# The adaLN matrix-vector product of a two-block kernel, moved to TensorE

## The chip, the cores and the metric

One Trainium2 chip, of which the kernel uses one core. The metric is the device time of one execution in microseconds (us). The kernel before takes 2879.64 us, the median of three runs (2877.4 to 2880.94).

## The reference

Two transformer blocks run one after the other on one sequence of 512 tokens with 1024 features, all in float32. The change concerns the first block alone, and in it the six conditioning vectors (adaLN), which come from one row `c` and a 1024 x 6144 matrix:

```python
ada = jax.nn.silu(c) @ w_ada + b_ada
shift1, scale1, gate1, shift2, scale2, gate2 = jnp.split(ada, 6, axis=-1)
h = modulate(rms_norm(x, norm1_g), shift1, scale1)      # h * (1 + scale) + shift
proj = h @ w_in + b_in                                  # attention and convolution branches
x = x + gate1[:, None, :] * mix
h2 = modulate(rms_norm(x, norm2_g), shift2, scale2)
x = x + gate2[:, None, :] * peer_layer(h2, ...)
```

Behind that come the PEER layer (a search over 16384 experts), and a second block with a Hyena filter, neighbourhood attention, pooling and a mixture of 16 experts.

## The kernel before

Activations are kept transposed: `X` holds 8 chunks of 128 features (partitions) by 512 tokens. So each of the 6 x 8 = 48 pieces of `ada` is a column of 128 numbers, used as a per-partition scale or shift. The host lays `w_ada` out in 24 groups of 1 MB. A group gives two columns of `ada`; for the first eight groups these are the shift and the scale of one feature chunk k.

`ada_group(g)` (L201) makes two columns. `c`, broadcast to all 128 partitions, stands in `cb` [128 x 1024] with the SiLU applied. Partition p of the group's tile holds the 1024 weights of output feature p, twice. For the first column, VectorE multiplies by `cb` and sums in one pass (L205). For the second, GpSimd multiplies (L206) and ScalarE sums while it copies (L207). VectorE adds the bias (L208). No TensorE instruction takes part.

`ada_load(g)` (L191) says where a group lies: groups 0 to 3 in the tiles `wide`, which later hold the filter's tables and the `mh`/`ml` of the output projection, group 6 in the room of `q_sb`, all others in two rotating buffers `wada`. All are loaded on SyncE's queue, which also carries `w_in`, `w_out` and all later weights, in order.

Around it the first block runs in these stages:

- The first stage loads `X`, forms the RMS norm (`nps`, `rps`), and then, chunk by chunk for k = 0 to 7: `ada_group(k)`, the scale `gs` (L233), `modulate` (L166 to L170: `mt` on VectorE, `mt` again and `hh` on ScalarE, `hl` on VectorE), and 15 matmuls that add chunk k to five blocks of the input projection in PSUM. Each product is made of three (`mm3`, L84): `hh` and `hl` are the high and low parts of the activations, `whi` and `wlo` those of the weights, which ScalarE and VectorE split (L81, L82).
- The second stage makes the Hyena filters of the second block (`hyena_filters`, two sine steps that pass between VectorE, ScalarE and TensorE) and the first attention scores (`ssp`, one PSUM tile of two banks) with their softmax.
- The third stage holds the other 13 blocks of the input projection, four attention blocks (`pt`, `op`, `nps`, `rps`), four convolution groups, `ada_group` 8 to 23, and the output projection (`mh`, `ml`).
- Behind it come a filter spectrum (`dw` loaded, L437), the second norm and the PEER layer.

The order of instructions inside these stages is not the order of the program. A scheduler puts each engine's instructions in an order of its own from the dependences, the buffers and a cost table. Each engine then runs its list strictly in that order; the same holds for SyncE's loads. Only the main loop of the PEER layer is written out by hand (`manual_schedule`).

Of the kernel before, what the change touches and what calls it, by code (L numbers as in the profile page):

```python
# [9 lines left out]
F32 = mybir.dt.float32  # L10
# [4 lines left out]
AF = mybir.ActivationFunctionType  # L15
ALU = mybir.AluOpType
# [4 lines left out]
P = 128  # L21
D = 1024
KD = 8
T = 512
# [11 lines left out]
def body(ctx, tc, I, O):  # L36
    nc = tc.nc
    mm = nc.tensor.matmul
    act = nc.scalar.activation
    vtt = nc.vector.tensor_tensor  # L40
    vts = nc.vector.tensor_scalar
    stt = nc.vector.scalar_tensor_tensor
    ptt = nc.gpsimd.tensor_tensor
# [4 lines left out]
    def const(name, shape, src=None, q=None, pool=None):  # L48
        t = (pool or cp).tile(shape, F32, name=name, tag=name)
        (q or nc.sync).dma_start(t, I[name] if src is None else src)  # L50
        return t
# [11 lines left out]
    ident = const("ident", [P, P], q=nc.scalar)  # L63
    ones = const("ones", [P, P], q=nc.scalar)
    hblk = const("hblk", [P, P], q=nc.scalar)
    cols = const("cols", [P, I["cols"].shape[1]], q=nc.scalar)
    eps_t = cp.tile([P, 1], F32, name="eps_t", tag="eps_t")
    nc.vector.memset(eps_t, EPS)
# [7 lines left out]
    def cols_of(name):  # L76
        o, n = CO[name]
        return cols[:, o:o + n]
# [83 lines left out]
    ada = cp.tile([P, 48], F32, name="ada", tag="ada")  # L162
# [14 lines left out]
    with ExitStack() as fx:  # L177
        fp = fx.enter_context(tc.tile_pool(name="fp", bufs=1))
        pp = fx.enter_context(tc.tile_pool(name="fps", bufs=2, space=PSUM))

        def mmp():
            return pp.tile([P, T], F32, name="mmp", tag="mmp", bufs=3)

        cb = fp.tile([P, D], F32, name="cb", tag="cb")
        a = I["c"]
        nc.scalar.dma_start(cb, bass.AP(tensor=a.tensor, offset=a.offset, ap=[[0, P], [1, D]]))
        act(cb, cb, AF.Silu)

        wide = [fp.tile([P, 2, 2, D], F32, name="wide", tag=tag) for tag in ("mh", "ml")]

        def ada_load(g):  # L191
            if g < 4:
                w = wide[g // 2][:, g % 2]
            elif g == 6:
                w = fp.tile([P, 2, D], F32, name="wq", tag="q_sb")
            else:
                w = fp.tile([P, 2, D], F32, name="wada", tag="wada", bufs=2)
            nc.sync.dma_start(w, I["w_ada"][g])
            return w

        def ada_group(g, w=None):  # L201
            if w is None:
                w = ada_load(g)
            b = 2 * g
            stt(w[:, 0], w[:, 0], 1.0, cb, op0=ALU.mult, op1=ALU.mult, accum_out=ada[:, b:b + 1])  # L205
            ptt(w[:, 1], w[:, 1], cb, op=ALU.mult)  # L206
            act(w[:, 1], w[:, 1], AF.Copy, accum_out=ada[:, b + 1:b + 2])  # L207
            vtt(ada[:, b:b + 2], ada[:, b:b + 2], cols_of("b_ada")[:, b:b + 2], op=ALU.add)  # L208

        hh = fp.tile([P, KD, T], F32R, name="hh", tag="hh")  # L210
        hl = fp.tile([P, KD, T], F32R, name="hl", tag="hl")
# [4 lines left out]
        with ExitStack() as ex:  # L216
            ep = ex.enter_context(tc.tile_pool(name="ep", bufs=1))
            ws0 = WStream(ep, I["w_in"], bufs=3, per=1, hbufs=NI)
            s1 = ep.tile([P, T], F32, name="s1", tag="s1")
            act(s1, X[:, 0], AF.Square)  # L220
            for k in range(1, KD):
                vtt(s1, s1, square(ep, X[:, k]), op=ALU.add)
            r1 = rms_t(ep, pp, [s1], D, False)
            wf, aw = [], []
            for i in range(4):
                wf += [ws0.get(b) for b in range(2 * i, min(2 * i + 2, NI))]
                aw.append(ada_load(i))
            early = [mmp() for _ in range(3)] + [pp.tile([P, T], F32, name="mmp", tag="pt", bufs=2) for _ in range(NI - 3)]
            for k in range(KD):
                ada_group(k, aw[k])  # L230
                if k + 4 < KD:
                    aw.append(ada_load(k + 4))
                stt(gs1[:, k:k + 1], ada[:, 2 * k + 1:2 * k + 2], 1.0, cols_of("norm1_g")[:, k:k + 1],  # L233
                    op0=ALU.add, op1=ALU.mult)
                modulate(k, r1, gs1[:, k:k + 1], ada[:, 2 * k:2 * k + 1], hh, hl, fp)
                for b in range(NI):
                    mm3(early[b], wf[b][0][:, k], wf[b][1][:, k], hh[:, k], hl[:, k], k == 0, k == KD - 1)
            q_sb = fp.tile([P, 4, T], F32, name="q_sb", tag="q_sb")
            for i in range(NI):
                act(q_sb[:, i] if i < 4 else k_sb, early[i], AF.Identity, bias=col("b_in", i))  # L240

        hyena_filters(nc, fp, mmp, I, pm)
        mh = fp.tile([P, KD, T], F32R, name="mh", tag="mh")
        ml = fp.tile([P, KD, T], F32R, name="ml", tag="ml")
# [5 lines left out]
        ps = mmp()  # L250
# [71 lines left out]
        for i in range(4):  # L322
            sc = attn_scores(i)
            conv_group(i)
            attn_out(*sc)
            if i == 1:
                for g in range(8, 12):
                    ada_group(g)
# [3 lines left out]
        for g in range(12, 20):  # L332
            ada_group(g)
        for i in range(KD):
            ps = mmp()
# [1034 lines left out]
def prep(inp):  # L1370
    g = {k: np.asarray(v) for k, v in inp.items()}
    A = {}

    def colv(v):
        return v.reshape(-1, P).T
# [3 lines left out]
        return w.reshape(KD, P, n, per, P).transpose(2, 1, 3, 0, 4)  # L1379

    A["xT"] = g["x"][0].T.reshape(KD, P, T).transpose(1, 0, 2)
    A["c"] = g["c"].reshape(1, D)
    A["ident"] = np.eye(P, dtype=np.float32)
    A["ones"] = np.ones((P, P), np.float32)
    A["hblk"] = np.kron(np.eye(2), np.ones((64, 64))).astype(np.float32)
    starts = [0, 16, 24, 32, 40, 44, 48, 52] + list(range(56, 64))
    A["start_row"] = np.tile(np.array(starts, np.float32), (P, 1))
    ao = np.array([k + 8 * s for k in range(8) for s in range(2)] + list(range(16, 48)))
    A["w_ada"] = g["w_ada"].T.reshape(48, P, D)[ao].reshape(24, 2, P, D).transpose(0, 2, 1, 3)
    hperm = [h for i in range(4) for h in (i, i + 4)]  # L1390
    qperm = np.concatenate([np.arange(64) + 64 * h for h in hperm])
    cgrp = [np.concatenate([1280 + np.arange(P) + P * i, 1792 + np.arange(P) + P * i, 768 + np.arange(P) + P * i])
# [6 lines left out]
    q = np.arange(P)[:, None]  # L1399
# [66 lines left out]
    for t_ in range(4):  # L1466
        kc0 = (0, 8, 24, 32)[t_]
        c = (16 * t_ + np.arange(P) // 8)[:, None]
# [36 lines left out]
```

## Time and profile before

| | us |
|---|---|
| median of three runs | 2879.64 |
| the runs | 2877.4, 2879.64, 2880.94 |
| span of the profiled execution (no other time is listed for it) | 2880.2 |
| TensorE busy in it | 2568.9 (89%) |
| VectorE busy | 1482.4 (51%) |
| ScalarE busy | 941.3 (33%) |
| GpSimd busy | 714.3 (25%) |

The span runs from the first to the last instruction of one execution. Busy times are shares of that whole span and say nothing of a single stage. The edited part lies in the first tenth of it, so the rows below go by stage. In the profile PE is TensorE, DVE is VectorE, ACT is ScalarE, POOL is GpSimd, and SP is SyncE, whose DMA issues are marked SPq. A plain float32 matmul of the program stands in the profile as two MATMUL records.

### The profile page before, as it was taken

What the parts mean: (1) busy time and instruction counts of PE and PEld (TensorE: products, weight loads), DVE (VectorE), ACT (ScalarE), POOL (GpSimd) and SP (SyncE); (2) the same over time, 40 slices, a digit from 0 to 9 for tenths busy, and PEclk for the clock granted to TensorE, in tenths of its full rate; (3) what the DMA queues carried; (4) which work ended last, traced back from release to release, by engine and by line L of the source; (5) the groups of instructions that cost most, each with busy time, mean ns of one, the idle gap of its engine ahead of it and who ended that gap; (6) DMA issues with size and microseconds to landing.
All of it is one profiled execution on the core that took longest, in us unless ns stands there. A gap on an engine that the chain in (4) does not pass through costs nothing.

```text
span 2880.2 us, 32762 instructions
## 1 busy us (share of the span) xinstructions
PE 2568.9 (89%) x12449; PEld 1816.3 (63%) x12449; DVE 1482.4 (51%) x2552; ACT 941.3 (33%) x1412; POOL 714.3 (25%) x427
## 2 busy tenths in 40 slices
PE   5798998799999999999999899969878878788787
PEld 4566888699888888899888777633323223232232
DVE  6863799984677778778777855330101101011011
ACT  5563436786333333333333434220000000000001
POOL 3411003575344444444444322110000000000000
PEclk9799999999999999999999999989999999999999
DMA  6622323457789989988989522289999999999997
GB/s 240 229 74 84 110 87 125 157 213 274 270 311 316 326 302 317 326 305 313 321 314 323 183 90 74 92 329 422 421 421 421 421 421 421 421 422 421 421 421 319
DMA packets 227813, 826.41 MB, mean 287 GB/s; under 512 B 19815, under 2 KB 88807, under 8 KB 175304
## 3 DMA queue, kind: packets, MB, share of 16 engines
q1 hardware_dynamic: 187448, 681.20, 61.2%
q0 software_dynamic: 38016, 138.43, 13.7%
q10 hardware_dynamic: 2192, 4.69, 0.4%
q8 instruction: 98, 1.61, 0.2%
q14 instruction: 59, 0.48, 0.0%
HBM read 787.02 MB, written 37.22 MB: 286 GB/s over the span
## 4 chain that ended last, share of the span: by engine, by line
PE 53%; DMA 32%; DVE 10%; ACT 2%; issue 2%; POOL 1%; SPq 0%; ACTq 0%; DVEq 0%; POOLq 0%
DMA wch<-in_w_up 10%; DMA wch<-in_w_gate 10%; DMA wch<-in_w_down 10%; PE acc L87 6%; PE acc L86 6%; PE acc L85 6%; PE aps L87 5%; PE aps L86 5%; PE aps L85 5%; PE mmp L85 4%; PE mmp L87 4%; PE mmp L86 4%; PE gps L583 2%; DMA uraw<-in_peer_uT 1%; PE upp L1297 1%
## 5 line engine op out<-in xcount | busy, mean ns | idle before, releaser
L1304 DVE TENSOR_TENSOR sg<-sg,upp 128x512 f32<-128x512 f32 x32 | 22.0, 688 | 765.8 <-PE upp L1297 765.8
L87 PE MATMUL aps<-hh,ulo 128*128 128x384 f32 x1024 | 346.6, 339 | 9.4 <-DVE ulo L401 6.3
L85 PE MATMUL aps<-hh,uhi 128*128 128x384 f32 x1024 | 348.1, 340 | 2.8 <-ACT uhi L400 1.8
L86 PE MATMUL aps<-hl,uhi 128*128 128x384 f32 x1024 | 347.1, 339 | 0.0
L1297 PE MATMUL upp<-wch,XB 128*64 128x512 f32 x1024 | 263.1, 601 | 61.8 <-DMA wch<-in_w_up 61.8
L1297 PE MATMUL gp<-wch,XB 128*64 128x512 f32 x1024 | 261.0, 600 | 47.3 <-DMA wch<-in_w_gate 47.2
L85 PE MATMUL acc<-vh,wh 128*128 128x512 f32 x768 | 299.6, 390 | 2.1 <-ACT wh L81 2.1
L87 PE MATMUL acc<-vh,wl 128*128 128x512 f32 x768 | 300.3, 391 | 0.0
L86 PE MATMUL acc<-vl,wh 128*128 128x512 f32 x768 | 299.6, 390 | 0.3 <-DVE vl L82 0.3
L625 POOL DMA_INDIRECT row<-in_peer_v,gidx x128 | 210.0, 1641 | 236.4 <-DVE gacc L638 208.8
L625 POOL DMA_INDIRECT row<-in_peer_u,gidx x128 | 199.8, 1561 | 264.6 <-DVE gscr L632 232.9
L1324 PE MATMUL y<-wch,aT 128*64 128x512 f32 x1024 | 246.1, 598 | 11.2 <-ACT aT L1313 11.2
L1297 PEld LDWEIGHTS upp<-wch,XB 128*64 128x64 f32 x1024 | 80.9, 137 | 224.5 <-DMA wch<-in_w_up 110.8
L1297 PEld LDWEIGHTS gp<-wch,XB 128*64 128x64 f32 x1024 | 81.0, 137 | 205.3 <-issue 114.8
L400 ACT ACTIVATE uhi<-uraw 128x1024 fp32r<-128x1024 f32 x128 | 135.6, 1059 | 206.5 <-DMA uraw<-in_peer_uT 141.4
L87 PEld LDWEIGHTS aps<-hh,ulo 128*128 128x128 f32 x1024 | 194.6, 190 | 12.2 <-DVE ulo L401 8.4
L85 PEld LDWEIGHTS aps<-hh,uhi 128*128 128x128 f32 x1024 | 194.9, 190 | 6.7 <-ACT uhi L400 2.0
L86 PEld LDWEIGHTS aps<-hl,uhi 128*128 128x128 f32 x1024 | 194.5, 190 | 4.0
L401 DVE TENSOR_TENSOR ulo<-uraw,uhi 128x1024 fp32r<-128x1024 f32 x114 | 149.8, 1314 | 80.0 <-ACT uhi L400 74.5
L1303 ACT ACTIVATE sg<-gp 128x512 f32<-128x512 f32 x32 | 19.1, 597 | 483.8 <-PE gp L1297 483.8
L1324 PEld LDWEIGHTS y<-wch,aT 128*64 128x64 f32 x1024 | 87.8, 136 | 136.5 <-issue 108.6
L81 ACT ACTIVATE vh<-vraw 128x1024 fp32r<-128x1024 f32 x128 | 134.6, 1052 | 94.8 <-PE acc L87 92.9
(406 smaller groups left out, 4586.1 us busy)
## 6 DMA issues: line engine op xcount, KB each, us to landing
wch<-in_w_gate SPq DMA_DIRECT2D x128, 1024.0 KB
wch<-in_w_up SPq DMA_DIRECT2D x128, 1024.0 KB
wch<-in_w_down SPq DMA_DIRECT2D x124, 1024.0 KB
uraw<-in_peer_uT SPq DMA_DIRECT2D x128, 512.0 KB
vraw<-in_peer_v SPq DMA_DIRECT2D x128, 512.0 KB
Gd<-st SPq DMA_DIRECT2D x48, 512.0 KB
gg<-Gd SPq DMA_DIRECT2D x16, 1536.0 KB
wada<-in_w_ada SPq DMA_DIRECT2D x19, 1024.0 KB
```

The source lines that it names most:

```text
L81: act(hi, src, AF.Copy)
L85: mm(out, lh, rh, start=first, stop=False)
L86: mm(out, lh, rl, start=False, stop=False)
L87: mm(out, ll, rh, start=False, stop=last)
L400: act(hi, raw, AF.Copy)
L401: lo_engine.tensor_tensor(lo, raw, hi.bitcast(F32), op=ALU.subtract)
L583: mm(ps[:, j], oq[:, 4 * t4 + j], of[:, 4 * t4 + j], start=True, stop=True)
L625: nc.gpsimd.indirect_dma_start(out=row, out_offset=None, in_=I[src], in_offset=bass.IndirectOffsetOnAxis(ap=gidx[:, j:j + 1], axis=0))
L1297: mm(ps[64 * e:64 * e + 64], xT[:, k, 64 * e:64 * e + 64], gu[w][k // 4][e][:, o:o + T], start=k == 0, stop=k == KD - 1)
L1303: act(sg, ps2[0], AF.Silu)
L1304: vtt(sg, sg, ps2[1], op=ALU.mult)
L1324: mm(y[c][64 * e:64 * e + 64], aT[:, fb, 64 * e:64 * e + 64], dn[fb // 2][e][:, o:o + T], start=fc == 0 and fb == 0, stop=fc == 3 and fb == 3)
```

## The change

`c` is no longer broadcast: it is loaded as `cs` [128 x 8], feature 128 k + p at partition p, column k. The weights of a group are laid out with the summed index on the partitions, 8 chunks of [128 x 256]. For each chunk k a matmul takes column k of `cs`, repeated 32 times, as the stationary operand, and streams the 256 weight columns. Chunks k and k + 4 write to the same strip of 32 PSUM partitions, so four strips hold four partial sums, each 32 times over. Then one copy brings [128 x 256] to SBUF as `arow` (ScalarE for groups 0 to 7, VectorE for the rest), and two matmuls with the 0/1 vector `sel4` sum one partition of each strip and turn the result into two columns. VectorE adds the bias from PSUM. The PSUM tile `adp` shares the one buffer of the attention scores `ssp`.

```diff
+    sel4 = const("sel4", [P, 1], q=nc.scalar)
-        cb = fp.tile([P, D], F32, name="cb", tag="cb")
-        nc.scalar.dma_start(cb, bass.AP(tensor=a.tensor, offset=a.offset, ap=[[0, P], [1, D]]))
-        act(cb, cb, AF.Silu)
+        cs = fp.tile([P, KD], F32, name="cs", tag="cs")
+        nc.scalar.dma_start(cs, I["c"])
+        act(cs, cs, AF.Silu)
...
-            stt(w[:, 0], w[:, 0], 1.0, cb, op0=ALU.mult, op1=ALU.mult, accum_out=ada[:, b:b + 1])
-            ptt(w[:, 1], w[:, 1], cb, op=ALU.mult)
-            act(w[:, 1], w[:, 1], AF.Copy, accum_out=ada[:, b + 1:b + 2])
-            vtt(ada[:, b:b + 2], ada[:, b:b + 2], cols_of("b_ada")[:, b:b + 2], op=ALU.add)
+            early = g < 8
+            ps = pp.tile([P, 2, T], F32, name="adp", tag="ssp", bufs=1)
+            for k in range(KD):
+                q = 32 * (k % 4)
+                mm(ps[q:q + 32, 0, :256], cs[:, k:k + 1].to_broadcast([P, 32]), w[:, k], start=k < 4, stop=k >= 4)
+            row = fp.tile([P, 256], F32, name="arow", tag="arow", bufs=2)
+            if early:
+                act(row, ps[:, 0, :256], AF.Copy)
+            else:
+                nc.vector.tensor_copy(row, ps[:, 0, :256])
+            for j in range(2):
+                mm(ps[:, 1, j:j + 1], row[:, j * P:(j + 1) * P], sel4, start=True, stop=True)
+            vtt(ada[:, b:b + 2], ps[:, 1, 0:2], cols_of("b_ada")[:, b:b + 2], op=ALU.add)
```

The tiles of `wide`, `wq` and `wada` change from [2, 1024] to [8, 256] per partition, the same size. The scheduler makes a new order on every engine up to the spectrum; the rows below are TensorE's, where the line numbers of the changed kernel are up to 10 higher.

In the first stage TensorE's list holds only projections. This is a piece of it before, from the middle of the eight chunks:

```order
L86 MATMUL mmp<-hl,whi 128x512
L87 MATMUL mmp<-hh,wlo 128x512
L85 MATMUL mmp<-hh,whi 128x512 x2
L86 MATMUL mmp<-hl,whi 128x512
L87 MATMUL mmp<-hh,wlo 128x512
```

The same place in the changed kernel, from the end of one chunk over group 5 and the start of the next chunk (`sel_78` is `sel4`):

```order
L88 MATMUL mmp<-hh,wlo 128x512
L216 MATMUL adp<-sel_78,arow 128x1 x2
L209 MATMUL adp<-wada,cs 32x256 x8
L86 MATMUL mmp<-hh,whi 128x512 x4
L87 MATMUL mmp<-hl,whi 128x512
L88 MATMUL mmp<-hh,wlo 128x512
```

The two `sel4` matmuls that finish the next chunk's columns, and the eight of the group after that, now stand between the chunks' projections.

At the end of the third stage TensorE before goes from the last projection to a norm sum and the spectrum:

```order
L87 MATMUL mmp<-mh,wlo 128x512
L119 MATMUL nps<-ones,sx 128x1
L437 MATMUL mmp<-pm,dw 128x256 x20
```

In the changed kernel four groups, 20 to 23, stand between the two:

```order
L88 MATMUL mmp<-mh,wlo 128x512
L209 MATMUL adp<-wada,cs 32x256 x8
L216 MATMUL adp<-sel_78,arow 128x1 x2
L209 MATMUL adp<-wada,cs 32x256 x8
L216 MATMUL adp<-sel_78,arow 128x1 x2
L209 MATMUL adp<-wada,cs 32x256 x8
L216 MATMUL adp<-sel_78,arow 128x1 x2
L209 MATMUL adp<-wada,cs 32x256 x8
L216 MATMUL adp<-sel_78,arow 128x1 x2
L446 MATMUL mmp<-pm,dw 128x256 x20
```

Before, the last groups' work on VectorE, GpSimd and ScalarE was done far ahead of this place; now the last four stand behind all projections.

## Rows read from the trace of the kernel before

**Rows 1.** Stretches: length; busy PE, PEld, DVE, ACT, POOL (instructions); PE clock; DMA; GB/s.

```profile
0.00:70.00 70.00, 38.76 (x137) 29.15 (x138) 49.05 (x67) 37.47 (x55) 28.77 (x14) 0.95 0.65 242
70.00:101.20 31.20, 17.52 (x51) 7.69 (x49) 29.05 (x49) 21.03 (x47) 11.06 (x4) 0.59 0.62 217
101.20:160.00 58.80, 54.41 (x247) 41.81 (x247) 49.86 (x62) 29.39 (x53) 28.11 (x10) 0.90 0.62 224
160.00:279.50 119.50, 113.11 (x563) 84.18 (x563) 53.07 (x82) 59.76 (x106) 9.04 (x8) 0.94 0.14 49
```

**Rows 2.** Timeline of TensorE, stage 1: start, duration, instruction, count, [idle before it].

```profile
19.03 2.07 PE L127 MATMUL rps<-ident,rt 128*128 128x128 f32 x8 [0.60 <-DVE rt L122]
25.57 2.07 PE L85 MATMUL mmp<-hh,whi 128*128 128x512 f32 x4 [4.46 <-ACT hh L169]
...
30.85 0.63 PE L87 MATMUL mmp<-hh,wlo 128*128 128x512 f32 x1
31.28 0.63 PE L86 MATMUL mmp<-hl,whi 128*128 128x512 f32 x1
...
69.24 0.39 PE L86 MATMUL mmp<-hl,whi 128*128 128x512 f32 x1
69.47 0.40 PE L87 MATMUL mmp<-hh,wlo 128*128 128x512 f32 x1
```

**Rows 3.** Timeline of VectorE and ScalarE, stage 1.

```profile
26.46 1.04 ACT L81 ACTIVATE whi<-wraw 128x1024 fp32r<-128x1024 f32 x1
...
46.85 0.15 DVE L208 TENSOR_TENSOR ada<-ada,cols 128x2 f32<-128x2 f32 x1
47.04 0.16 DVE L233 SCALAR_TENSOR_TENSOR gs<-ada,cols 128x1 f32<-128x1 f32 x1
47.11 1.22 DVE L205 SCALAR_TENSOR_TENSOR wada<-wada,cb 128x1024 f32<-128x1024 f32 x1
47.23 0.82 ACT L168 ACTIVATE mt<-mt,ada,gs 128x512 f32<-128x512 f32 x1 [0.71 <-DVE gs L233]
48.08 0.63 ACT L169 ACTIVATE hh<-mt 128x512 fp32r<-128x512 f32 x1
```

**Rows 4.** Timeline of TensorE, stage 3 and the spectrum.

```profile
172.20 1.94 PE L286 MATMUL op<-pT,v_sb 128*64 128x512 f32 x8
...
175.56 1.01 PE L119 MATMUL nps<-hblk,sq 128*128 128x2 f32 x8
...
300.47 3.83 PE L437 MATMUL mmp<-pm,dw 128*128 128x256 f32 x17
```

**Rows 5.** Timeline of VectorE, stages 2 and 3.

```profile
79.81 2.33 DVE L140 TENSOR_TENSOR m<-m,sinks 128x8 f32<-128x8 f32 x1
...
82.67 1.79 DVE L142 TENSOR_SCALAR nm<-m 128x8 f32<-128x8 f32 x1
...
98.99 0.15 DVE L142 TENSOR_SCALAR nm<-m 128x8 f32<-128x8 f32 x1
...
153.77 0.74 DVE L313 SCALAR_TENSOR_TENSOR cv<-z,cols,cv 128x512 f32<-128x512 f32 x1
...
157.86 2.83 DVE L314 SCALAR_TENSOR_TENSOR cv<-z,cols,cv 128x512 f32<-128x512 f32 x1
```

**Rows 6.** Waits of TensorE, 130 to 170 us: total, times, longest.

```profile
PE nps L119 <- ACT sq L133: 5.3, 2, 2.9
```

**Rows 7.** Timeline of several engines: a short pass, a `wada` load, the stage's end.

```profile
74.21 0.41 DVE L271 SCALAR_TENSOR_TENSOR s<-ssp,amask 128x256 f32<-128x256 f32 x1
...
86.73 3.23 SPq L198 DMA_DIRECT2D wada<-in_w_ada  x2
...
91.60 2.35 POOL L206 TENSOR_TENSOR wada<-wada,cb 128x1024 f32<-128x1024 f32 x1 [7.17 <-DMA wada<-in_w_ada]
...
279.15 0.39 PE L87 MATMUL mmp<-mh,wlo 128*128 128x512 f32 x1
...
286.10 11.21 PE L437 MATMUL mmp<-pm,dw 128*128 128x256 f32 x40 [5.20 <-DMA dw<-in_dft]
```

More of the change, by code (lines that the diff above doesn't have):

```diff
@@ L182, in mmp @@
             return pp.tile([P, T], F32, name="mmp", tag="mmp", bufs=3)
-        cb = fp.tile([P, D], F32, name="cb", tag="cb")
-        a = I["c"]
-        nc.scalar.dma_start(cb, bass.AP(tensor=a.tensor, offset=a.offset, ap=[[0, P], [1, D]]))
-        act(cb, cb, AF.Silu)
-        wide = [fp.tile([P, 2, 2, D], F32, name="wide", tag=tag) for tag in ("mh", "ml")]
+        cs = fp.tile([P, KD], F32, name="cs", tag="cs")
+        nc.scalar.dma_start(cs, I["c"])
+        act(cs, cs, AF.Silu)
+        wide = [fp.tile([P, 2, KD, 256], F32, name="wide", tag=tag) for tag in ("mh", "ml")]
         def ada_load(g):
@@ L194, in ada_load @@
             elif g == 6:
-                w = fp.tile([P, 2, D], F32, name="wq", tag="q_sb")
+                w = fp.tile([P, KD, 256], F32, name="wq", tag="q_sb")
             else:
-                w = fp.tile([P, 2, D], F32, name="wada", tag="wada", bufs=2)
+                w = fp.tile([P, KD, 256], F32, name="wada", tag="wada", bufs=2)
             nc.sync.dma_start(w, I["w_ada"][g])
@@ L1381, in prep @@
     A["xT"] = g["x"][0].T.reshape(KD, P, T).transpose(1, 0, 2)
-    A["c"] = g["c"].reshape(1, D)
+    A["c"] = colv(g["c"])
+    A["sel4"] = (np.arange(P) % 32 == 0).astype(np.float32).reshape(P, 1)
     A["ident"] = np.eye(P, dtype=np.float32)
@@ L1388, in prep @@
     ao = np.array([k + 8 * s for k in range(8) for s in range(2)] + list(range(16, 48)))
-    A["w_ada"] = g["w_ada"].T.reshape(48, P, D)[ao].reshape(24, 2, P, D).transpose(0, 2, 1, 3)
+    A["w_ada"] = (g["w_ada"].reshape(KD, P, 48, P)[:, :, ao].reshape(KD, P, 24, 256).transpose(2, 1, 0, 3))
     hperm = [h for i in range(4) for h in (i, i + 4)]
```

## The prediction

> **What bounds the kernel now.** I read the time by stage first. The edit touches only work before about 286 us; up to there the table of stages [rows 1] is to be read for which engine has holes. In the first 70 us TensorE is busy 38.8 us, from 70 to 101.2 only 17.5 of 31.2, while VectorE is busy 29.05 of those 31.2: that stretch belongs to VectorE. From 101.2 on TensorE sets the pace: 54.4 of the first 58.8 us and 113.1 of the next 119.5. So the change takes work from the engine that bounds 31 us and gives it to the one that bounds the 178 us behind it.
>
> Next the timeline, to find where each stage ends. Stage 1 ends with the last early projection matmul at 69.9 [rows 2]. Stage 2 is the hyena filters and the first softmaxes. Stage 3, the remaining projections, ends at 279.5, and TensorE's next stage, the spectrum, begins at 286.1 after a wait of 5.2 us for the `dw` load [rows 7]. From the middle of the spectrum's matmuls on, the order of TensorE's instructions is the same before and after, and none of the edited tiles is used there except as a finished column. So I carry what is gained or lost at that point to the end, one for one.
>
> **What one group costs on TensorE.** Eight matmuls stream 256 columns each into four column strips of 32, in plain f32; the profile shows two matmul records for each such program line, so 16 records x 256 = 4096 columns. The nearest row is `op` [rows 4]: 8 records x 512 columns, also 4096, alternating between two column strips, 1.94 us. Above: with no two strips at once, the spectrum's full-width row gives 17 records of 256 columns in 3.83, so 16 take 3.6 us. Below: all four strips at once would be a quarter of that, 0.9 us. I take 1.9: the two records of one f32 matmul go to the same strip one behind the other, so with four strips as with two, only the last record of one matmul and the first of the next can overlap. The two `sel4` matmuls have four records; `nps` [rows 4] has eight such in 1.01, so 0.5. A group is 1.9 + 0.5 = 2.4 us, 24 groups 57.6 us.
>
> The row bears a factor of 3.6/1.94 = 1.9. The Trainium skill, "TensorE: Matmul & The Clock Gate", section "Measured speedup vs the span model", gives 2.38 for three column strips and 3.07 for four row strips: by it a group's eight would take an estimated 1.2 us, 0.7 less. No row here has four strips in use, so that is a rival below and not the sum.
>
> **What is removed.** 24 passes over 128x1024 on each of three engines: 1.22 us apiece on VectorE (L205, [rows 3]), about the same on ScalarE (L207, of the size of the `whi` row there, 1.04), and 2.35 or more on GpSimd (L206, [rows 7]), which does little else before 160 us. The broadcast load of `c` (512 KB) becomes one of 4 KB, against which ScalarE's queue issues one load more; I cost both at nothing, since the first squares of `X` cover them. With the passes goes something larger per piece: while GpSimd runs, short VectorE instructions are stretched, such as a 128x8 `m` of 2.33 us and an `nm` of 1.79 where the same `nm` undisturbed takes 0.15 [rows 5].
>
> **Stage 1 (0 to 70): +9.** In the new order TensorE gets, for each of eight chunks k, two `sel4` matmuls for k, eight matmuls for group k+1, then the 15 projection matmuls of k. The projections of k need `hh` of k, which now starts from the `sel4` result. So between one chunk's last projection and the next chunk's first stands a chain: `sel4` 0.5, `ada` 0.15, `gs` 0.16, `mt` 0.82, `hh` 0.63 [rows 3], with about 0.2 of hops = 2.5 us. Group k+1 (1.9) lies inside it at no cost; if it took 3.6, it would be the longer branch. Then 15 x 0.23 = 3.45 [rows 2]. (The 0.23 and, below, 0.43 are start to start, at the high and the low of the clock's two levels, 2.4 and 1.2 GHz, 69.24 to 69.47 and 30.85 to 31.28 in [rows 2].) A period is 5.9; before, the modulate chain ran ahead of TensorE and a chunk cost 3.4 where GpSimd didn't disturb it. The start: `rps` ends at 21.1 [rows 2]; group 0 at the low clock 2 x 1.9, copy to SBUF 0.5, `sel4` 1.0, `ada` and `gs` 0.3, `mt` 0.82, a `whi` split that stands between (1.04, [rows 3]), `hh` 0.63, hops 0.2: first projection at 29.4, where it was 25.6. The second chunk: 12 matmuls at 0.43, group 1, two more, the chain, so near 40. That is where it was before, since the old second chunk sat behind GpSimd. Six more periods of 5.9 and the last 3.45: 79, against 69.9. The bounds: TensorE's own work without the chain's waits saves about 0.6 a chunk (+4); 3.6 us groups give +21.
>
> **Stage 2 (70 to 101.2): -5.** VectorE loses four L205 passes here (4.9 us) and the stretch of one `nm` (1.6) and of two `m` (2.2 each, with the undisturbed `nm` for a short 128x8 step): 10.9 of its 29. Not all of it stands on the path, which is two sine chains that pass from VectorE to ScalarE and back, with table loads that stay; two thirds, 7.3, is my choice, since VectorE is busy nearly throughout. Against it, five matmuls of group 8 now stand ahead of the filter's last matmuls, at the low clock (the stage's granted clock is 0.59) 5/8 of 3.8 = 2.4. Ends: -11 and +2.4.
>
> **Stage 3 (101.2 to 279.5): +24.** Twelve groups (8 to 19) at 2.4 = 28.8. Each has a copy from PSUM on VectorE between its two parts (0.41, the 128x256 row in [rows 7]) with only one to seven matmuls in between, and group g+1 may not start until `ada` of g has read the one PSUM buffer: 0.4 of stall a group, 4.8. TensorE has 4.4 + 6.4 = 10.8 us idle here, and loses 0.10 x 58.8 + 0.06 x 119.5 = 13.1 us to the low clock [rows 1]. Of the idle time 5.3 is `nps` waiting for `sq` [rows 6], which stands behind a `cv` stretched to 2.83 that takes 0.74 undisturbed [rows 5]: 4 comes back. Of the clock I give back nearly half, 6, since a stage with more to do has fewer gaps. 28.8 + 4.8 - 10 = 23.6. Ends: 12 x 1.4 - 23.9 = -7 (four strips at once, every hole filled) and 12 x 4.5 = +54.
>
> **The end of the stage: +7.** Groups 20 to 23 now stand alone behind the last projection. Group 22's buffer is free when group 20's matmuls have read it, 1.9 after the end; a `wada` load is used 4.9 after its issue (86.73 to 91.60, [rows 7]), so it lands at 6.8. Group 23's load follows group 21 and lands near 10; with 1.9, the copy, `sel4` and hops the spectrum begins at about 13.2. It began 286.1 - 279.5 = 6.6 behind the last projection, waiting for `dw`, which is now hidden under the groups. Ends: +3 and +16 (3.6 us groups, or `dw` held up as well).
>
> **Sum.** 9 - 5 + 24 + 7 = +35. The profiled execution's span is 2880.2; nothing but the span is listed for it, and the slowest run is 2880.94, so under 1 us lies around it. The median of the runs shown is 2879.64, 0.6 below the span. 2880.2 + 35 = 2915.
>
> **Rivals.**
> 1. *All four strips overlap.* A group's eight cost 1.0. For it: the strips are separate, and two of them do overlap. Against: the order of records within an f32 matmul. Stage 1 loses only its slow start (-2), stage 3 falls by 12 x 0.9 = 11, the end by 3: +19, so 2899. By the page named above, at 1.2, it would be an estimated 2902.
> 2. *No overlap.* 3.6 a group, say because the moving data differs from strip to strip, which in `op` it also does (against it). Stage 1 gains 12 more, stage 3 20, the end 7: +74, 2954.
> 3. *VectorE was the real bound up to 170, and TensorE's holes swallow the new work.* For it: VectorE is busy 128 of the first 160 us, much of that stretched by GpSimd; TensorE's holes from its first projection to the spectrum (about 10 + 13.7 + 10.8 + 6) and the lost clock (13) make 53 us, near the 57.6 added. It decides if a group costs under 53/24 = 2.2 and the holes can be reached. At 1.5 a group (36 us) it gives 17 back at best, 2863; half of that, 2872, is its likely time. Against: holes that come from a wait don't go when work is put ahead of that wait, and the `sel4` chain makes new ones.
>
> **How the numbers follow.** Forecast 0.54 (alone 2895 to 2935), rival 1 0.21, rival 2 0.11, rival 3 0.14. The range 2885 to 2955 leaves out rival 3 and half of rival 2, some 0.19. About 0.2% (5.8 us) is what a measurement can tell from no change. Rival 3 is faster in 0.10 and no change in 0.04, rival 1 falls into no change in 0.03: faster 0.10, same 0.07, slower 0.83.
>
> **What would show it.** The eight `adp` matmuls of a group take 1.8 to 2.0 from first start to the next instruction (rival 1: 1.0 to 1.2; rival 2: 3.6). The first projection stands at about 29, the last early one at about 79, chunks 5.9 apart with `hh` as their releaser. Stage 2 shrinks to about 26 us, with no VectorE instruction of 128x8 over 0.3. The spectrum's first matmul stands near 321 instead of 286, and behind that the two traces run in step. I am wrong if stage 1 ends before 70, if TensorE's idle time in stage 3 falls under 5 us, or if the difference at the spectrum is not the difference at the end.

## The result and the profile after

The changed kernel takes 2897.75 us, the median of 4 runs (2895.72 to 2900.66). The kernel before took 2879.56 us in the same comparison (median of 4, 2877.4 to 2880.94). The ratio is 1.0061, with a 95% interval of 1.0049 to 1.0072: 18 us slower. The forecast was 2915 us, 35 us slower, so the sign held and the size was twice what came.

The stages first, for the changed kernel; the columns are those of [rows 1], and the four stretches are cut where its own stages end: the last early projection, the first projection behind the softmaxes, the last projection, and the spectrum's first matmul.

```profile
0.00:77.60 77.60, 49.93 (x297) 35.62 (x298) 24.66 (x47) 30.10 (x46) 0.20 (x4) 1.00 0.58 212
77.60:103.70 26.10, 18.45 (x54) 7.49 (x54) 17.29 (x32) 14.37 (x29) 0.00 (x0) 0.60 0.23 81
103.70:283.30 179.60, 178.52 (x1051) 129.62 (x1051) 82.31 (x139) 77.20 (x142) 8.79 (x7) 0.99 0.35 121
283.30:300.20 16.90, 9.65 (x82) 5.45 (x81) 4.18 (x11) 1.41 (x2) 0.21 (x1) 0.62 0.70 249
```

Set beside the kernel before, cut at the same events (all in us):

| | before | after | difference | forecast |
|---|---|---|---|---|
| stage 1 ends | 69.87 | 77.55 | +7.7 | +9 |
| stage 2 lasts | 31.26 | 26.18 | -5.1 | -5 |
| stage 3 lasts | 178.41 | 179.61 | +1.2 | +24 |
| last projection to spectrum | 6.56 | 16.82 | +10.3 | +7 |
| spectrum starts | 286.10 | 300.16 | +14.1 | +35 |

From the spectrum's first matmul to the end both spans need the same: 2880.2 - 286.1 = 2594.1 before, 2893.9 - 300.2 = 2593.7 after. In these two executions, what is lost up to there is carried to the end one for one. Over all kept traces of this document that rest takes between 2591.0 and 2598.2 us, so elsewhere a difference at the spectrum is that of the whole kernel to within some us. The two profiled executions are 13.7 us apart and the medians 18.2, because a profiled execution is one draw: that of after took 2895.72 us, 2.0 under its median; with the same 1.8 us around the span, that of before lay an estimated 2.4 over its own.

Now the four places. In stage 1, TensorE's timeline of the changed kernel over one period (start, duration, instruction, count, idle before it and its releaser):

```profile
26.56 1.22 PE L86 MATMUL mmp<-hh,whi 128*128 128x512 f32 x2 [2.83 <-ACT hh L170]
...
46.96 0.50 PE L216 MATMUL adp<-sel,arow 128*128 128x1 f32 x4
47.78 1.07 PE L209 MATMUL adp<-wada,cs 128*32 128x256 f32 x16 [0.32 <-DVE ada L217]
49.48 1.19 PE L86 MATMUL mmp<-hh,whi 128*128 128x512 f32 x4 [0.63 <-ACT hh L170]
...
53.03 0.50 PE L216 MATMUL adp<-sel,arow 128*128 128x1 f32 x4
53.86 1.07 PE L209 MATMUL adp<-wada,cs 128*32 128x256 f32 x16 [0.32 <-DVE ada L217]
55.56 1.21 PE L86 MATMUL mmp<-hh,whi 128*128 128x512 f32 x4 [0.63 <-ACT hh L170]
```

The reader is to see two things. The projections start every 6.1 us (49.48 to 55.56), and 2.5 of these pass from the `sel4` matmuls to the first projection, with `hh` as releaser: the chain that was forecast. And the eight matmuls of a group, 16 records, take 1.07 us.

In stage 3, the waits of TensorE (total, times, longest) are nearly gone. Before, they held the 5.3 us of [rows 6] and, beside smaller ones, the two that stand first here; the other three are all that is left after:

```profile
PE mmp L85 <- ACT mh L81: 1.9, 1, 1.9
PE mmp L87 <- DVE wlo L82: 1.8, 1, 1.8
```

```profile
PE adp L216 <- DVE arow L214: 0.5, 1, 0.5
PE adp L209 <- DVE ada L217: 0.3, 1, 0.3
PE pt L292 <- ACT pT L293: 0.2, 1, 0.2
```

Behind the last projection, TensorE's timeline of the changed kernel; then what VectorE does in those 3.82 us; then, from the list of DMA issues, the load of group 22 issued at 284.74 (KB, us from issue to landing):

```profile
283.27 1.07 PE L209 MATMUL adp<-wada,cs 128*32 128x256 f32 x16
285.32 0.61 PE L216 MATMUL adp<-sel,arow 128*128 128x1 f32 x4 [0.99 <-DVE arow L214]
286.18 1.07 PE L209 MATMUL adp<-wada,cs 128*32 128x256 f32 x16 [0.25 <-DVE ada L217]
287.80 1.01 PE L216 MATMUL adp<-sel,arow 128*128 128x1 f32 x4 [0.55 <-DVE arow L214]
292.63 1.93 PE L209 MATMUL adp<-wada,cs 128*32 128x256 f32 x16 [3.82 <-DVE stb L435]
295.10 1.01 PE L216 MATMUL adp<-sel,arow 128*128 128x1 f32 x4 [0.54 <-DVE arow L214]
296.37 1.94 PE L209 MATMUL adp<-wada,cs 128*32 128x256 f32 x16 [0.25 <-DVE ada L217]
300.16 1.19 PE L446 MATMUL mmp<-pm,dw 128*128 128x256 f32 x2 [0.30 <-issue]
```

```profile
288.85 0.16 DVE L217 TENSOR_TENSOR ada<-adp,cols 128x2 f32<-128x2 f32 x1 [1.10 <-PE adp L216]
291.29 1.23 DVE L435 CAST stb<-start_row 128x2048 bf16<-128x2048 f32 x1 [2.28 <-DMA start_row<-in_start_row]
```

```profile
wada<-in_w_ada SPq DMA_DIRECT2D x1, 1024.0 KB, 7.8
```

Each group waits out a copy and an `ada`, and before group 22 TensorE stands still for 3.8 us. The label names the cast of `stb`, but the matmuls read nothing of it, and the `ada` that frees their PSUM buffer ended at 289.0. They also wait for their weights: issued when group 20's matmuls had read the buffer, landed at 284.74 + 7.8 = 292.5. The cast happened to end in the same tenth of a microsecond, and a wait for several things is put down to the last. The mean granted clock of this stretch is 0.62, and behind that wait its last groups run at the lower of the two levels, 1.2 GHz: 1.94 us instead of 1.07, `sel4` 1.01 instead of 0.5.

Last, the short steps of VectorE after (count; shortest, median and longest in ns; first and last start): no 128x8 `m` or `nm` above 0.17 us, where [rows 5] had 1.79 and 2.33.

```profile
L143 DVE TENSOR_SCALAR nm<-m x8: 157/171/174, 86.8 to 1808.6; 128x8 f32<-128x8 f32 x8
L141 DVE TENSOR_TENSOR m<-m,sinks x4: 156/158/168, 86.6 to 195.0; 128x8 f32<-128x8 f32 x4
```

### The profile page after: what moved, and what is told of

Read it like the earlier page. It is cut to its first block, busy times and chain, and to the rows that moved or that the text cites. A ratio compares the mean times of both kernels' runs of the same rounds, so it can differ in the third digit from the quotient of the medians.

```text
span 2893.9 us, 33614 instructions
## 1 busy us (share of the span) xinstructions
PE 2601.0 (90%) x12929; PEld 1831.7 (63%) x12929; DVE 1426.9 (49%) x2520; ACT 915.3 (32%) x1370; POOL 654.5 (23%) x403
## 4 chain that ended last, share of the span: by engine, by line
PE 58%; DMA 31%; DVE 8%; ACT 2%; issue 1%; POOL 1%; SPq 0%; ACTq 0%; DVEq 0%; POOLq 0%
DMA wch<-in_w_up 10%; DMA wch<-in_w_down 10%; DMA wch<-in_w_gate 9%; PE acc L88 6%; PE acc L87 6%; PE acc L86 6%; PE aps L87 5%; PE aps L88 5%; PE aps L86 5%; PE mmp L86 4%; PE mmp L88 4%; PE mmp L87 4%; PE gps L592 2%; PE upp L1306 1%; PE y L1333 1%
## 5 line engine op out<-in xcount | busy, mean ns | idle before, releaser
L647 DVE SCALAR_TENSOR_TENSOR gacc<-row,ga,gacc 128x1024 f32<-128x1024 f32 x128 | 164.1, 1282 | 2.3
```

Of the source, the lines that this page charges most:

```text
L647: stt(outp, row, ga[:, n - P:n - P + 1], outp, op0=ALU.mult, op1=ALU.add)
```

## The experiments

Two readings stood against each other for stage 3, where 22 us less was lost than forecast. Theory A: GpSimd's products were slowing VectorE's steps, and taking them away gave the time back. Theory B: the groups' matmuls fill holes of TensorE, whatever GpSimd does. Besides these, the price of a group and the two chains were to be tested. All stages below are cut at the events of the table.

**gp_kept.** The changed kernel, with a GpSimd product over each late group's weights whose result nobody uses.

```diff
+            if not early:
+                scr = fp.tile([P, 4, 256], F32, name="scr", tag="scr")
+                ptt(scr, w[:, 0:4], w[:, 4:8], op=ALU.mult)
```

> The changed kernel, with a GpSimd product of 128x1024 (result unused) added to each of the 16 groups from 8 on; TensorE's order is the same as in the changed kernel. Theory A (contention): the third stage kept its 179.6 us because GpSimd no longer stretches VectorE's short steps. Then its idle time (1.1 us) goes back towards 10.8 and its granted clock (0.99) towards 0.93: 10 to 20 us longer, 2908 to 2918. Theory B (filler): the ada matmuls themselves fill the holes and keep the clock up. Then the stage stays within 2 us of 179.6 and the time near 2898 to 2900.

2904.55 us, 1.0073 [1.0057, 1.0090] of the kernel before. Its stage 3, in the columns of [rows 1]:

```profile
107.90:289.90 182.00, 178.79 (x1051) 129.47 (x1054) 92.75 (x139) 77.23 (x142) 38.50 (x19) 0.99 0.35 119
```

GpSimd is busy 38.5 us again and VectorE 92.8 for the same instructions, 10.4 more than after, but the stage grows by only 2.4 us, so the expectation from theory A missed. The run doesn't refute the theory, though: in this order none of the stage's 12 products starts before 162 us, and no 128x8 step and no division of a softmax is stretched (0.20 and 2.29 us at most); the stretch falls on other steps, such as two `cv` (2.09 and 2.88). That stretch costs little because VectorE is half idle here and TensorE has work left is a reading, not shown by itself.

Stage 1 grew by 3.9 as well, and there the trace shows a stretched step on the path. First the last chunk's first projection after, then `gs` and that projection in gp_kept:

```profile
73.82 1.20 PE L86 MATMUL mmp<-hh,whi 128*128 128x512 f32 x4 [2.02 <-ACT hh L170]
```

```profile
72.31 2.31 DVE L245 SCALAR_TENSOR_TENSOR gs<-ada,cols 128x1 f32<-128x1 f32 x1
76.18 2.01 PE L86 MATMUL mmp<-hh,whi 128*128 128x512 f32 x4 [4.17 <-ACT hh L170]
```

A product runs from 72.3 to 74.6; `gs` beside it takes 2.31 us instead of 0.16, TensorE waits 2.15 longer for `hh`, and the chunk's first matmuls behind that wait run at the low level of the clock, which makes the chunk 1.6 longer.

**no_late.** The changed kernel without the matrix-vector work of groups 8 to 23; their columns get the bias and two of the weights, a wrong result. The weights are still loaded.

```diff
+            if not early:
+                vtt(ada[:, b:b + 2], w[:, 0, 0:2], cols_of("b_ada")[:, b:b + 2], op=ALU.add)
+                return
```

> The changed kernel, which leaves out the matrix-vector product of groups 8 to 23 (the bias and two weights are added instead; the weights are still loaded). So neither the filler nor GpSimd's work is there. Theory A (contention): the third stage has no holes to fill and shrinks by the groups' own 21 us to about 158, and the end by 10: about 2867. Theory B (filler): without the filler the holes are back, idle 8 to 11 us and a clock near 0.93, so the third stage takes 170 to 178: 2880 to 2888.

2868.10 us, 0.9953 [0.9936, 0.9969]. Its stage 3:

```profile
100.80:265.20 164.40, 158.81 (x809) 120.72 (x808) 77.22 (x118) 70.37 (x123) 8.90 (x7) 0.98 0.28 100
```

That splits the +1.2: without the groups the stage takes 164.4, 14.0 less than before; with them 179.6, 15.2 more. The twelve groups add 178.5 - 158.8 = 19.7 us of busy time to TensorE; 15.2 of it shows, and 4.5 falls into holes (idle 5.6 without the groups, 1.1 with them). So both theories hold a part, and A's is the larger, as far as no_late can tell GpSimd's absence from that of the passes. The wait for `mh` shows B's part: it is 1.9 us in no_late, as before, and gone in the changed kernel.

**no_gp** and **no_gp_kept.** Theory A by itself, on the kernel before: for groups 8 to 23 VectorE does both columns, in two passes instead of one, and GpSimd and ScalarE none. In the second kernel GpSimd's product is put back behind it, its result unused, and ScalarE's pass is not.

```diff
-            ptt(w[:, 1], w[:, 1], cb, op=ALU.mult)
-            act(w[:, 1], w[:, 1], AF.Copy, accum_out=ada[:, b + 1:b + 2])
+            if g < 8:
+                ptt(w[:, 1], w[:, 1], cb, op=ALU.mult)
+                act(w[:, 1], w[:, 1], AF.Copy, accum_out=ada[:, b + 1:b + 2])
+            else:
+                stt(w[:, 1], w[:, 1], 1.0, cb, op0=ALU.mult, op1=ALU.mult, accum_out=ada[:, b + 1:b + 2])
+                # in no_gp_kept alone:
+                ptt(w[:, 1], w[:, 1], cb, op=ALU.mult)
```

> The kernel before, with both columns of groups 8 to 23 made by VectorE's multiply and sum (16 more passes of 1.22 us), none by GpSimd and ScalarE. Theory A (contention): the stretched steps are gone, TensorE's idle time in the third stage falls under 4 us and its clock rises to 0.97 or more; the stage shrinks from 178 to 160 to 166, 2860 to 2868. Theory B (filler): VectorE has more to do and TensorE no more than before, so the holes stay: 2878 to 2888.

> The kernel before with both columns of groups 8 to 23 made by VectorE, as in no_gp, and GpSimd's 16 products added again with a result that nobody uses. It separates what no_gp took away: GpSimd's use of SBUF beside VectorE, or ScalarE's 16 summing passes and their waits. If GpSimd stretching VectorE's steps was the cost, the third stage goes from 167 back to 175 to 180 and the second from 27.5 to 30 or more: 2878 to 2888. If it was ScalarE's passes, the stages stay within 3 us of no_gp: 2868 to 2872.

no_gp: 2868.43 us, 0.9949 [0.9932, 0.9965]. no_gp_kept: 2877.14 us, 0.9989 [0.9979, 0.9999]. Stages 2 and 3 of no_gp, then of no_gp_kept:

```profile
69.00:96.50 27.50, 18.39 (x52) 8.42 (x51) 23.54 (x46) 14.11 (x28) 0.00 (x0) 0.57 0.55 191
96.50:263.70 167.20, 159.11 (x809) 120.81 (x808) 104.17 (x179) 77.15 (x142) 8.90 (x7) 0.97 0.36 123
```

```profile
68.90:100.40 31.50, 18.79 (x53) 8.79 (x53) 28.21 (x46) 14.17 (x29) 8.04 (x3) 0.58 0.48 166
100.40:278.60 178.20, 164.63 (x809) 124.99 (x808) 121.77 (x179) 77.40 (x142) 42.63 (x20) 0.93 0.34 116
```

VectorE and ScalarE do the same work in both. With GpSimd's unused products stage 2 lasts 31.5 instead of 27.5, stage 3 178.2 instead of 167.2, the same as before the change, and VectorE is busy 121.8 us with what takes it 104.2 alone. ScalarE's passes are gone in both, so the difference isn't theirs. Nor is it that the products hold the weight buffers longer: in stage 3 TensorE waits for no load in either kernel, and VectorE 0.5 us for `wada` in no_gp_kept against 0.9. How the loss of the kernel before divides is less sure: there ScalarE's passes waited 10.9 us for GpSimd's products in stage 3, and no run takes only that away.

Half of the 11.0 us of stage 3 are waits: TensorE is idle 13.6 us with the products and 8.1 without. The other half is the clock: the same 809 records are busy 164.6 us at a granted 0.93 and 159.1 at 0.97. Two of the waits in stage 3 (total, times, longest), no_gp and then no_gp_kept:

```profile
PE nps L119 <- ACT sq L133: 1.0, 1, 1.0
PE pt L286 <- DVE s L152: 0.5, 1, 0.5
```

```profile
PE nps L119 <- ACT sq L133: 5.5, 3, 4.7
PE pt L287 <- DVE s L152: 3.4, 1, 3.4
```

The second wait is for the softmax's division; that step, from 69 us to the end of stage 3, first in no_gp and then in no_gp_kept (busy us, mean ns):

```profile
L152 DVE TENSOR_TENSOR s<-s,den 128x2048 f32<-128x2048 f32 x3 | 6.9, 2285 | 0.0
```

```profile
L152 DVE TENSOR_TENSOR s<-s,den 128x2048 f32<-128x2048 f32 x3 | 10.6, 3537 | 0.1
```

The Trainium skill, "SBUF — State Buffer", section "Terms", says that VectorE and GpSimd arbitrate for one port pair, which the one holds for a whole instruction while the other fully blocks. The traces agree: a step of 2285 ns becomes 3537 on the mean, one of 128x8 at most 2350, while a product of GpSimd takes 2.6 us. Here it is a matter of when a step starts: `cv` keeps its length in no_gp_kept (752 ns at most), where none of its steps that read `z` starts while a product runs, and takes 2825 in the kernel before, beside one.

Stages 2 and 3 together are 15 us longer in no_gp_kept, the kernel by the medians 9: in these two profiled executions no_gp's rest, from the spectrum on, took 4.3 us longer. Why it did isn't known.

**one_strip** and **two_strips.** The changed kernel with a group's matmuls over all 128 columns of the array, or in two strips of 64, `sel4` adapted.

```diff
-                q = 32 * (k % 4)
-                mm(ps[q:q + 32, 0, :256], cs[:, k:k + 1].to_broadcast([P, 32]), w[:, k], start=k < 4, stop=k >= 4)
+                # one_strip:
+                mm(ps[:, 0, :256], cs[:, k:k + 1].to_broadcast([P, P]), w[:, k], start=k == 0, stop=k == 7)
+                # two_strips, with q = 64 * (k % 2):
+                mm(ps[q:q + 64, 0, :256], cs[:, k:k + 1].to_broadcast([P, 64]), w[:, k], start=k < 2, stop=k >= 6)
```

> The changed kernel with the eight matmuls of a group all in one full-width strip, so that none can overlap. By the prediction's row (3.6 us) a group's eight take 3.4 to 3.6 instead of 1.07. Stage 1: a period of 7.5 instead of 6.1, 10 us more. Third stage: 12 x 2.5 = 30 more if no holes are left to fill, less if there are. End: 10 more. Sum 45 to 50, about 2945. If a group's length did not matter (hidden behind waits), 2900.

> The changed kernel with the eight matmuls of a group in two column strips of 64 instead of four of 32. If the prediction's row for two strips (op) was read rightly and only its step from two strips to four was wrong, a group's eight take 1.9 to 2.0, between 1.07 for four and 3.6 for one; the third stage grows by 12 x 0.9 = 11, the end by 3 to 4, the first stage by 2: near 2914. If two strips overlap no better than one, 2939.

one_strip: 2939.32 us, 1.0202 [1.0185, 1.0219]. two_strips: 2922.9 us in one run, without an interval. A group in each, from TensorE's timeline, one_strip and then two_strips:

```profile
322.03 3.62 PE L208 MATMUL adp<-wada,cs 128*128 128x256 f32 x16
```

```profile
302.39 1.95 PE L209 MATMUL adp<-wada,cs 128*64 128x256 f32 x16
```

3.62, 1.95, 1.07 us for one, two and four strips. A single record is as long in all three (count; shortest, median, longest in ns; the 19 groups in `wada`):

```profile
L208 PE MATMUL adp<-wada,cs x304: 377/379/763, 51.2 to 343.5; 128*128 128x256 f32 x152
```

```profile
L209 PE MATMUL adp<-wada,cs x304: 379/379/689, 50.4 to 321.1; 128*64 128x256 f32 x152
```

```profile
L209 PE MATMUL adp<-wada,cs x304: 378/380/637, 47.8 to 297.7; 128*32 128x256 f32 x152
```

So the records of different strips overlap: against one strip, a group is 1.9 times as fast with two and 3.4 times with four. (Its weight loads get shorter too, 190, 137 and 109 ns by the median, but by less.) With groups of 1.95, stage 3 is 7.7 us longer than after (187.29) and with 3.62 23.7 longer (203.34). The expectation for two_strips missed in stage 1, which grew by 11.4: the scheduler's order moved as well. It puts the last two of a group's 16 records behind the chunk's projections, so that the copy, hidden there in the changed kernel, joins the chain, and a period takes 7.56. In one_strip eight of the 16 stand there; its three parts came out at 15.0, 23.7 and 6.3 where 10, 30 and 10 were expected.

**tail, pipe, pipe_tail.** Two new orders of the changed kernel, alone and together, that take the chains off the path. tail puts groups 20 to 23 ahead of the output projection, pipe puts group k+1 ahead of the projections of k, pipe_tail does both.

```diff
-            for g in range(12, 20):
+            for g in range(12, 24):
...
-        for g in range(20, 24):
-            ada_group(g)
```

```diff
+            ada_group(0, aw[0])
             for k in range(KD):
-                ada_group(k, aw[k])
...
                 modulate(k, r1, gs1[:, k:k + 1], ada[:, 2 * k:2 * k + 1], hh, hl, fp)
+                if k + 1 < KD:
+                    ada_group(k + 1, aw[k + 1])
```

> The changed kernel with groups 20 to 23 called before the output projection instead of behind it. If the end's 16.8 us come from the four groups that stand alone there, the end falls to about 6.5 and the third stage grows by 4 x 1.5 = 6: 4 us less, 2893 to 2894. If the end is set by something else (the load of dw or start_row), the end stays near 16 and the time at 2898 or above.

> The changed kernel with ada_group(k+1) called before the 15 projection matmuls of chunk k instead of after them, so that the chain from sel4 to hh runs beside matmuls. If that chain sets the period of 6.1 us a chunk in the first stage, the period falls to TensorE's own 3.45 + 1.0 + 0.5 = 5.0 to 5.2 and the first stage from 77.5 to 70 to 71.5: 6 to 7 us less, 2891 to 2892. If TensorE's own work or the weights' arrival sets it, nothing changes: 2898.

> Both edits of pipe and tail in the changed kernel. If the first stage's chain and the end's four groups are separate places on one path, the gains add up: 7.6 and 4.7 below 2897.75, so 2885 to 2886, still 5 us above the kernel before. If one covers the other, 2890.

tail: 2893.08 us, 1.0044 [1.0027, 1.0060]. The last projection to the spectrum falls from 16.8 to 5.8 us, the four groups cost 6.9 in stage 3, 1.7 each. pipe: 2890.15 us, 1.0034 [1.0021, 1.0046]; stage 1 ends at 69.85. A period of pipe on TensorE's timeline:

```profile
45.89 1.07 PE L209 MATMUL adp<-wada,cs 128*32 128x256 f32 x16
...
47.70 0.50 PE L216 MATMUL adp<-sel,arow 128*128 128x1 f32 x4
48.06 0.48 PE L86 MATMUL mmp<-hh,whi 128*128 128x512 f32 x1
...
51.00 1.07 PE L209 MATMUL adp<-wada,cs 128*32 128x256 f32 x16
```

The `sel4` matmuls now stand among the projections, next to no wait is left (0.2 us), and the period is 5.1 instead of 6.1. pipe_tail: 2884.66 us, 1.0013 [1.0003, 1.0022]; the two gains add up. Even so the change is no gain over the kernel before.

**no_gp_all.** no_gp for all 24 groups: the matrix-vector product on VectorE alone.

> The kernel before with both columns of all 24 groups made by VectorE, none by GpSimd and ScalarE. If GpSimd's use of SBUF is what costs, the first stage gains too, since its second chunk stood behind stretched steps until 39: 3 to 6 us less than no_gp, 2862 to 2866. If VectorE's 8 more passes (10 us) fall on the first stage's path, it is 2870 to 2876.

2849.62 us, 0.9898 [0.9881, 0.9914]: 30 us less than before, and the best of all. Its first and third stage:

```profile
0.00:56.60 56.60, 36.13 (x137) 27.53 (x137) 43.75 (x86) 29.32 (x38) 0.20 (x4) 1.00 0.81 301
...
84.30:247.70 163.40, 158.03 (x809) 119.34 (x808) 101.77 (x174) 76.97 (x142) 8.88 (x7) 0.98 0.35 120
```

Stage 1 ends 13.2 us earlier than before, stage 3 is 15.0 shorter. That stage 3 is as short as in no_late, where the late groups aren't computed at all: VectorE does 23 passes more at no cost in that stage. In stage 1 GpSimd's and ScalarE's passes were not taken away one by one, but the trace of the kernel before shows where most of the 13 us went. Two VectorE steps and a wait of TensorE there, then the same `gs` in no_gp_all:

```profile
27.38 2.83 DVE L170 TENSOR_TENSOR hl<-mt,hh 128x512 fp32r<-128x512 f32 x1
35.78 2.26 DVE L233 SCALAR_TENSOR_TENSOR gs<-ada,cols 128x1 f32<-128x1 f32 x1
39.23 0.80 PE L87 MATMUL mmp<-hh,wlo 128*128 128x512 f32 x1 [4.34 <-DVE wlo L82]
```

```profile
28.99 0.15 DVE L232 SCALAR_TENSOR_TENSOR gs<-ada,cols 128x1 f32<-128x1 f32 x1
```

GpSimd's products follow one another from 26.6 to 41.4, and beside them VectorE's steps are stretched: `hl` takes 2.83 and `gs` 2.26 us, where no_gp_all has 0.69 and 0.15. From the first projection to the end of the stage TensorE waits 4.4 us for `hl`, 4.3 for `wlo` and 0.9 for `hh`, where no_gp_all has 0.2; the first projection comes 1.4 earlier there, and 2.6 us less busy time goes with a granted clock of 1.00 instead of 0.95. ScalarE's pass for the second chunk had ended at 26.5, so it held nothing up there.

## Why the prediction was right in sign and twice too large

**Stage 1 (+9 forecast, +7.7 measured): right in the mechanism, with sizes that partly cancel.** The first projection came at 26.6, not 29.4, and the second chunk at 36, not 40; then one period took 7.4, where the scheduler splits a group, and the others 6.1, not 5.9, so that the last one ended at 77.6, not 79. pipe shows the reason: with the chain out of the path the 7.7 us are gone.

**Stage 2 (-5, -5.1): right, and for the reason given.** no_late splits it: 6.8 less without the late groups, and 1.7 more with them, for a forecast of 7.3 and 2.4. no_gp gets 3.7 of it by freeing GpSimd (and ScalarE) alone, although VectorE carries more passes; no_gp_kept loses it again.

**Stage 3 (+24, +1.2): here the prediction failed,** in three terms.

- *12 x 2.4 = 28.8 for the groups.* The step that failed is "the two records of one f32 matmul go to the same strip one behind the other, so with four strips as with two, only the last record of one matmul and the first of the next can overlap". A group's eight take 1.07, not 1.9, and one_strip and two_strips show the overlap of 1.9 and 3.4. The row that the price was read from, `op` in [rows 4], was a true price for two strips (two_strips: 1.95), but not for four. The bound below, 0.9, and rival 1's 1.0 were near. The `sel4` matmuls take 0.5 as forecast. Twelve groups add 19.7 us, 9 less. The Trainium skill, "TensorE: Matmul & The Clock Gate", section "Measured speedup vs the span model", has 2.38 for three column strips and 3.07 for four row strips; the estimate of 1.2 us from it came out nearer than the row did, and the 3.4 here lies above both.
- *12 x 0.4 = 4.8 of stall.* The waits show 0.8. The scheduler's order seems to have left enough projections between a group's two parts; no run tests that.
- *10 returned (4 of holes, 6 of clock).* 19.3 came back (19.7 + 0.8 - 1.2). TensorE's idle time fell from 10.8 to 1.1, and the granted clock, 0.90 and 0.94 in [rows 1], is 0.99. By no_late 14.0 of it comes from the absence of GpSimd's products and the other passes (5.2 of idle time and 8.8 of busy time at a higher clock); the other 5.3 are the groups' matmuls in the holes that were left. So holes gave 10.5 where 4 were forecast, and the clock 8.8 where 6 were. The forecast looked at one wait alone, `nps` for `sq`, where the other waits for VectorE's and ScalarE's results went with it.

These misses, 9.1 + 4.0 + 9.3, make the 22.4 between 23.6 and 1.2. The prediction named the sign of its own failure: it was to be wrong if TensorE's idle time in stage 3 fell under 5 us.

**The end (+7, +10.3): right in kind, short by 3.** The groups' chain was forecast, with the wait of group 22 for a buffer and its load. Two sizes were off. The load landed 292.5 - 283.3 = 9.2 us behind the last projection, not 6.8: it took 7.8 instead of the 4.9 of [rows 7], with `dw` and a load of 1 MB for the next part issued in the 1.4 us ahead of it and the DMA engines busy 0.70 of the stretch. And the last two groups' `sel4` pairs ran at 1.2 GHz, 0.5 more each; the eights at that clock took 1.93 and 1.94, which the sum's 1.9 met by chance. 2.4 + 1.0 is nearly the 3.6 between 13.2 and 16.8. tail shows the price of the place: 11.0 us less there, for 6.9 more in stage 3.

**The sum's base (2880.2).** The prediction put under 1 us around the span. The runs list 1.7 to 1.9 for nearly every execution, so the profiled execution of the kernel before was, by that, a slower draw, and the base stood 0.6 above the median: a small part of the miss.

**The rivals.** Rival 1 (2899) had the group's price right, 1.07 for its 1.0, and came within 2 us, but partly by luck: it foresaw 12 too much in stage 3, where it too gave back only 10, and 6 too little at the end. Rival 2, no overlap, is one_strip: 2939. Rival 3, that TensorE's holes swallow the new work, was right in stage 3, where 19.7 us of matmuls cost 1.2. It failed on the places with nothing to swallow: the chain of stage 1 and the end of stage 3, 18 us together. pipe_tail takes these two away and still ends 4 us above the kernel before, not at 2863. The bound that rival 3 named, VectorE stretched by GpSimd, is borne out by no_gp_all: with GpSimd's products (and ScalarE's passes) gone, VectorE does more passes, the kernel is 30 us faster, and TensorE needn't carry a matmul for it.

## What to carry to other kernels

When an engine is busy for most of a stretch, first ask how much of that is its own work and how much is stretch from a neighbour: compare the longest and shortest time of one form in the groups by shape, then take the neighbour away before you move work to the engine that paces the stages behind. When work is added to the pacing engine, price it by rows with the same layout (strips, widths, records), keep the low bound as a live case where no such row exists, and look for holes in all waits of the stage and in its clock, not in the largest wait alone. Work that stands behind the last user of a full engine costs its whole chain, copies and loads included; put it ahead, where it cost little more than its busy time here (1.7 us a group in tail, for 1.07 + 0.5).

## What the runs showed of the hardware that was not expected

- Eight f32 matmuls of 128x256 (16 records of 0.38 us) take 3.62 us in one strip, 1.95 in two strips of 64 columns and 1.07 in four of 32: 1.9 and 3.4 times as fast, although each matmul has two records for one strip.
- The 1 MB `wada` load took 7.8 us from issue to landing behind the last projection, among other loads, where one in [rows 7] was used 4.9 after its issue.
- GpSimd's 16 products, unused, lengthen VectorE's busy time in stages 2 and 3 by 22 us (150.0 against 127.7) for the same instructions, and the kernel by 9 us (2877.14 against 2868.43).
- 12 unused products cost only 2.4 us in stage 3 of the changed kernel (gp_kept), while one of them beside a single 128x1 step that TensorE's chain waits for cost most of 3.9 us in stage 1.
- Half of the 11.0 us that the products cost stage 3 in no_gp_kept shows as waits of TensorE, the other half as a lower granted clock (0.93 against 0.97).
